# Block products by seven multiplications in the recurrence's projections as well

## The chip, the cores and the metric

The kernel runs as one program on one core of a Trainium2 chip. The metric is the time on the device of one execution, in microseconds (us), the median of several. The core's engines run their own instruction streams and wait for each other on semaphores: TensorE (PE: matmuls and transposes), VectorE (DVE), ScalarE (ACT), GpSimd (POOL), and the DMA queues, all issued here by SyncE (SP). Matmul operands and other tiles lie in SBUF; matmuls write the eight banks of PSUM, each of 128 rows by 512 fp32 numbers.

## What is computed

One step of a decoder layer with d = 1024, for a prompt of 1024 tokens with 16 learned tokens ahead, and for 8 single sample tokens that carry their own state. The core of the reference:

```
xn   = rmsnorm(h, norm_pre)
proj = xn @ w_in                                   # (L, 1024) @ (1024, 10 * 1024)
q, fr, i_in, z_a, b_g, c_g, h_c, z_b, gate_a, gate_b = split(proj)
f    = lb + (1 - lb) * sigmoid(fr);  k = 1 - f;  qa = silu(q)
o    = hgrn_mix(qa, k, i_in, log f)                # 8 heads: S_t = diag(f_t) S_{t-1} + k_t v_t^T ; o_t = q_t^T S_t
o    = rmsnorm(o, hgrn_norm) * silu(z_a);          y_a = o @ w_a
u    = c_g * h_c;  conv = causal width-3 depthwise convolution of u
y_b  = (b_g * conv * silu(z_b)) @ w_b
out  = (sigmoid(gate_a) * y_a + sigmoid(gate_b) * y_b) @ w_o
h    = h + rmsnorm(out, norm_post)
```

Outputs are h for prompt and sample tokens, the recurrence's last states and the convolution's last inputs.

## The kernel before, in words

**Layout.** Channels lie on the partitions and tokens on the free axis. The 1048 tokens are two halves of 524 columns (even 128-token chunks, odd chunks; 4 sample tokens and 8 learned ones at each end). Every fp32 operand of a large product is held as two fp32r parts, a high part (cast on ACT, L85) and the low rest (subtraction, on DVE unless told otherwise, L86: `split`). One block product is three matmuls, high-high, high-low and low-high (`mm3`, L109 to L111). The normalised input lies in SBUF as four blocks b00, b01, b10, b11 (channel half, token half), each as four 128-row pieces.

**Stages.** (1) A prelude loads, normalises and transposes the input (`prep`, L171 on PE) between the four projections of head 0. (2) For head m, a generator `hgrn(m)` of 19 steps is woven into `projections(m + 1)`: four sections of w_in (i, f, q, z), each of four column chunks with 8 pieces and three matmuls, so 4 x 4 x 24 = 384 matmuls per head. `weave` puts a step of the recurrence behind every so many half chunks. Head 7 runs beside four plain gate sections of the same size. (3) Two more plain gate sections run beside `block_sums`, which forms from the four blocks, high and low added on POOL (L592), subtracted on DVE (L595 to L600) and split again, the factors t1 to t4 of Winograd's form of the 2 x 2 block product. (4) `strassen` computes 21 pairs of sections by that form: seven block products in place of eight. The pairs are those of the convolution branch (c and h; b and z_b, eight each) and five pairs of gates. Per product j and pair, POOL and DVE prepare an operand (sums of weight blocks in `add`, L628 to L631; split in `operand`), three products ahead of its use; results pile up in PSUM banks pa, pb, pc, are saved to SBUF (`sc`, L667) or added from there (DVE, from PSUM, L711 to L768). (5) Two products with w_a and w_b, the output product and the residual.

**The recurrence.** One head's steps: two transposes of i (V, L235) and a small one; a front of DVE work on K, X (silu of q) and F (L260 to L263, with a split) that ends in two sums on PE (L271, L272) and one more (L361); seven levels, each with a copy on ACT (L364), four matmuls (L366), two products and one masked write on DVE (L368, L369, L374); then transposes of K, the states (L420 on DVE), the reads (L431, L433), a norm (squares on ACT, L436; root on POOL, L77 and L78; scaling on DVE, L441) and two transposes out (L447, L448). The sample tokens' states are updated in levels 1 to 6 (L316 to L346).

**What sets the order.** Each engine runs its instructions in the order of the program after scheduling; a tile of a pool waits until the last user of its buffer is done. Buffers: 6 operand buffers w, 4 raw weight buffers wr, two buffers each for X, F, K, ZS, 4 + 4 PSUM banks.

## Time and profile before

| | |
|---|---|
| median of 3 runs | 1327.33 us (1325.76 to 1327.61) |
| profiled execution, its own time | 1323.88 us |
| its span, first to last instruction | 1322.1 us, mean granted TensorE clock 0.997 |
| PE busy | 1293.5 us (98%) |
| DVE, ACT, POOL busy | 771.5 (58%), 433.0 (33%), 295.2 us (22%) |
| chain of waits by engine | PE 90%, DVE 6%, POOL 1%, DMA 1%, ACT 1% |

The profile comes from one execution, whose own time is 1.8 us above its span and 3.4 us below the median of the runs. The page divides the span into 40 slices and gives the busy tenths of each engine in them; a window view does the same for stretches that one names. The chain of waits is followed back from the last instruction: at each step to what released it. A line of a helper (L86, L109) stands for all its callers, so groups are told apart by tiles.

### The profile page before, as it was taken

The page shows a single profiled execution, that of the slowest core. Times are in us where ns is not written, and L with a number is a line of the kernel's source. Part 1 is how long each engine was busy: PE and PEld are TensorE (multiplying, and loading weights), DVE is VectorE, ACT ScalarE, POOL GpSimd, SP SyncE. Part 2 cuts the span into 40 slices and gives each one's busy share as a digit, 9 for nine tenths or more (in the row PEclk, how much of TensorE's full clock was granted, in tenths as well). Part 3 has the DMA queues.
Part 4 walks back from the last instruction along what each step waited for, and adds up shares of the span by engine and source line. Part 5 has one row for each costly group of instructions (what it writes and reads, how often), then busy time and mean ns, then how long its engine had stood idle before and what let it go on. Part 6 is the DMA issues. An engine that isn't in the chain of part 4 may idle for free.

```text
span 1322.1 us, 24885 instructions
## 1 busy us (share of the span) xinstructions
PE 1293.5 (98%) x10409; PEld 1259.5 (95%) x10409; DVE 771.5 (58%) x1336; ACT 433.0 (33%) x959; POOL 295.2 (22%) x372
## 2 busy tenths in 40 slices
PE   6999999999999999998999999999999999999997
PEld 5999999999999999998999999999999999999876
DVE  5397767776767676659655656655544523535052
ACT  6233333233232323234333334333445402213031
POOL 4121110202020201067554344353330000000010
PEclk9999999999999999999999999999999999999999
DMA  9022212131312121222212222213324833521141
GB/s 274 19 80 67 81 51 81 51 96 36 112 45 87 51 81 51 97 83 64 66 49 80 65 66 77 64 52 97 124 85 150 301 98 113 176 89 57 32 146 48
DMA packets 134590, 117.07 MB, mean 89 GB/s; under 512 B 3953, under 2 KB 119770, under 8 KB 134478
## 3 DMA queue, kind: packets, MB, share of 16 engines
q1 hardware_dynamic: 134478, 115.49, 28.1%
q8 instruction: 81, 1.33, 0.4%
q14 instruction: 31, 0.25, 0.1%
HBM read 89.48 MB, written 25.96 MB: 87 GB/s over the span
## 4 chain that ended last, share of the span: by engine, by line
PE 90%; DVE 6%; POOL 1%; DMA 1%; ACT 1%; issue 1%; SPq 0%; DVEq 0%; POOLq 0%; ACTq 0%
PE g L109 19%; PE g L110 18%; PE g L111 18%; PE h L111 8%; PE h L110 8%; PE h L109 8%; PE h L366 3%; PE h L433 1%; PE h L431 1%; PE h L414 1%; DVE w L86 1%; PE h L171 1%; PE h L447 1%; PE h L397 1%; DMA it<-in_x_prompt_dram 0%
## 5 line engine op out<-in xcount | busy, mean ns | idle before, releaser
L85 ACT CAST w<-wr 128x512 fp32r<-128x512 f32 (+1 forms) x116 | 94.8, 817 | 221.4 <-PE h L110 93.9
L86 DVE TENSOR_TENSOR w<-wr,w 128x512 fp32r<-128x512 f32 (+1 forms) x114 | 127.0, 1115 | 58.5 <-ACT w L85 58.5
L109 PE MATMUL g<-b00h,w 128*128 128x256 f32 (+1 forms) x448 | 131.8, 296 | 5.5 <-ACT z L564 5.1
L110 PE MATMUL g<-b00l,w 128*128 128x256 f32 (+1 forms) x448 | 128.2, 286 | 0.0
L111 PE MATMUL g<-b00h,w 128*128 128x256 f32 (+1 forms) x448 | 128.0, 286 | 0.0
L109 PE MATMUL g<-b10h,w 128*128 128x256 f32 (+2 forms) x440 | 125.8, 286 | 0.0
L110 PE MATMUL g<-b10l,w 128*128 128x256 f32 (+2 forms) x440 | 124.7, 283 | 0.0
L111 PE MATMUL g<-b10h,w 128*128 128x256 f32 (+2 forms) x440 | 124.4, 283 | 0.0
L109 PE MATMUL g<-b01h,w 128*128 128x256 f32 (+3 forms) x416 | 119.4, 287 | 0.0
L110 PE MATMUL g<-b01l,w 128*128 128x256 f32 (+3 forms) x416 | 117.9, 283 | 0.2 <-DVE b01l L86 0.2
L111 PE MATMUL g<-b01h,w 128*128 128x256 f32 (+3 forms) x416 | 117.8, 283 | 0.0
L109 PE MATMUL g<-b11h,w 128*128 128x256 f32 (+3 forms) x384 | 112.1, 292 | 0.0
L110 PE MATMUL g<-b11l,w 128*128 128x256 f32 (+3 forms) x384 | 108.8, 283 | 0.0
L111 PE MATMUL g<-b11h,w 128*128 128x256 f32 (+3 forms) x384 | 108.7, 283 | 0.0
L109 PEld LDWEIGHTS g<-b00h,w 128*128 128x128 f32 x448 | 86.0, 193 | 8.8 <-ACT z L564 5.4
L110 PEld LDWEIGHTS g<-b00l,w 128*128 128x128 f32 x448 | 86.1, 192 | 0.8 <-DVE b00l L86 0.2
L111 PEld LDWEIGHTS g<-b00h,w 128*128 128x128 f32 x448 | 86.0, 192 | 0.0
L109 PEld LDWEIGHTS g<-b10h,w 128*128 128x128 f32 x440 | 83.0, 189 | 0.4 <-issue 0.2
L110 PEld LDWEIGHTS g<-b10l,w 128*128 128x128 f32 x440 | 83.0, 189 | 0.1
L111 PEld LDWEIGHTS g<-b10h,w 128*128 128x128 f32 x440 | 82.9, 188 | 0.0
L110 PEld LDWEIGHTS g<-b01l,w 128*128 128x128 f32 x416 | 78.5, 189 | 0.6 <-DVE b01l L86 0.6
L109 PEld LDWEIGHTS g<-b01h,w 128*128 128x128 f32 x416 | 78.6, 189 | 0.1
(631 smaller groups left out, 3990.1 us busy)
## 6 DMA issues: line engine op xcount, KB each, us to landing
wr<-in_w_in_dram SPq DMA_DIRECT2D x79, 512.0 KB
oz<-z SPq DMA_DIRECT2D x8, 516.0 KB
ga<-z SPq DMA_DIRECT2D x8, 516.0 KB
ob<-t SPq DMA_DIRECT2D x8, 516.0 KB
gb<-z SPq DMA_DIRECT2D x8, 516.0 KB
z<-ga SPq DMA_DIRECT2D x8, 516.0 KB
z<-gb SPq DMA_DIRECT2D x8, 516.0 KB
sin<-in_state_hgrn_dram SPq DMA_DIRECT2D x8, 512.0 KB
```

Source lines behind the costliest of these rows:

```text
L85: act.copy(hi, src)
L86: (eng or vec).tensor_tensor(out=lo, in0=src, in1=hi.bitcast(F32), op=ALU.subtract)
L109: pe.matmul(pt, wh, xh, start=first, stop=False, skip_group_check=onto)
L110: pe.matmul(pt, wh, xl, start=False, stop=False, skip_group_check=onto)
L111: pe.matmul(pt, wl, xh, start=False, stop=last, skip_group_check=onto)
L171: pe.transpose(pt[:, 128 * k:128 * k + rows], src, ident[0:rows, 0:rows])
L366: pe.matmul(pt[:, 128 * j:128 * j + 128], kms[:, ko + 128 * j:ko + 128 * j + 128], comp(X, 128 * j + B, nb // 4, HL - B, B), start=True, s ...
L397: pe.transpose(pt[:, 128 * j:128 * j + 128], K[:, c0:c0 + 128], ident)
L414: pe.matmul(pt[:, 128 * j:128 * j + 128], KT[:, 128 * i:128 * i + 128], V[:, 128 * i:128 * i + 128], start=True, stop=True)
L431: pe.matmul(o, A[:, c:c + 128], V[:, c:c + 128], start=True, stop=False)
L433: pe.matmul(o, X[:, cx:cx + 128], states[t], start=False, stop=True)
L447: pe.transpose(pt[:, 128 * j:128 * j + 128], onb[:, 512 * g + 128 * j:512 * g + 128 * j + 128], ident)
```

## The change

All seven factors of the input are formed in the prelude and stay in SBUF (s0 to s6, high and low). The recurrence's projections of heads 1 to 7 become pairs too, (i, f) and (q, z), and so do all gates: one stream of 38 pairs (14 of heads, 8 of gates, 16 of the convolution branch) runs through `strassen`, and `weave` puts the steps of `hgrn(m)` between its chunks, 28 chunks per head. Head 0 stays plain. To make room there are now three operand buffers w, two wr, and one each for F, K and i (X and ZS keep two); operands are prepared two products ahead; PSUM is split into two banks ga, two banks gb and four for the recurrence. In the head pairs the low parts of three of seven operands are made on POOL, and so is the product of q's silu (three of four chunks from SBUF sums); K is one ACT instruction. The sample tokens' state update leaves `hgrn`; its inputs are kept, and its 64 steps run between the chunks of the convolution's pairs.

```
-    psg = ctx.enter_context(tc.tile_pool(name="psg", bufs=4, space=bass.MemoryType.PSUM))
+    psg = ctx.enter_context(tc.tile_pool(name="psg", bufs=2, space=bass.MemoryType.PSUM))
...
-    BUFS = {"x": 2, "f": 2, "k": 2, "zs": 2, "z": 2, "w": 6, "wr": 4, "cs": 2, "sc": 2, "st": 5}
+    BUFS = {"x": 2, "zs": 2, "w": 3, "wr": 2, "sm": 3, "cs": 2, "sc": 2, "st": 5}
...
+    def whole(h, l, out):
+
+        pool.tensor_tensor(out=out, in0=h.bitcast(F32), in1=l.bitcast(F32), op=ALU.add)
...
+                if (kk, h) == (0, 1):
+                    r = slot("sm", 512)
+                    rv = cap(r, 0, [[n, 4], [1, n]])
+                    whole(cap(b11[0], c0, here), cap(b11[1], c0, here), rv)
+                    vec.tensor_tensor(out=rv, in0=src, in1=rv, op=ALU.subtract)
+                    src = rv
+                split(src, cap(hi, c0, here), cap(lo, c0, here))
...
+    def q_out(m, h, c0, n, pt, s):
+        out = of_head(m, "x", h, c0, n)
+        y = added(pt, s)
+        sg = sigmoid(y, n)
+        (vec if s is None else pool).tensor_tensor(out=out, in0=y, in1=sg, op=ALU.mult)
...
+        K = slot("k")
+        act.activation(out=K, in_=F, func=AF.Copy, scale=-1.0, bias=1.0)
+        for i, t in enumerate((F, X, ZS)):
+            pool.tensor_copy(cap(smpv, 32 * m + 8 * i, [[4, 2], [1, 4]]), cap(t, 512, [[HL, 2], [1, 4]]))
...
+    t2, t3, t4 = factor(2), factor(4), factor(5)
+    for k in range(4):
+        ab, c = slot(("kt", "s")[k % 2], 2 * HL), slot("sc", HL)
+        a, b = ab[:, 0:HL], ab[:, HL:2 * HL]
+        whole(*at(b22, k), a)
+        whole(*at(t1, k), b)
+        vec.tensor_tensor(out=a, in0=a, in1=b, op=ALU.subtract)
+        split(a, *at(t2, k))
+        whole(*at(b11, k), b)
+        vec.tensor_tensor(out=b, in0=a, in1=b, op=ALU.subtract)
+        split(b, *at(t3, k))
+        whole(*at(b21, k), c)
+        vec.tensor_tensor(out=c, in0=c, in1=a, op=ALU.subtract)
+        split(c, *at(t4, k))
+        if k == 0:
+            groups(gi(1, 1), gf(1, 1))
+        if k == 1:
+            groups(gq(1, 1), gz(1, 1))
...
-    for m in range(7):
-        weave(projections(m + 1, tiles), 32, run_hgrn(m), N_HG, 1 if m else 2)
...
-    weave(gates_plain(0, 1, 2, 3), 32, run_hgrn(7), N_HG)
...
-    weave(gates_plain(4, 5), 16, block_sums(), 16)
...
-                sa, sb_ = (slot(t, 1024) for t in (("kt", "s"), ("a", "ee"))[p % 2])
-                s1, s2, s3, s4 = sums[p] = sa[:, 0:512], sa[:, 512:1024], sb_[:, 0:512], sb_[:, 512:1024]
+                s1, s2, s3 = sums[p] = [slot("sm", HL)[:, 0:512] for _ in range(3)]
...
+                s1, s2, s3 = sums.get(p, (None,) * 3)
+                src = (quad(p, 0, 0), quad(p, 0, 1), s2, s1, s3, quad(p, 1, 1), s2)[j]
                 w = ops[i] = slot("w", 1024, F32R)
-                split(src, w[:, 0:512], w[:, 512:1024])
+                split(src, w[:, 0:512], w[:, 512:1024], pool if j in pairs[p][2] else vec)
+                if j == 2:
+                    pool.tensor_tensor(out=s2, in0=quad(p, 0, 1), in1=s2, op=ALU.subtract)
 
         load(0)
-        load(1)
+        operand(0)
+        operand(1)
         add(0)
-        for i in range(3):
-            operand(i)
...
-        for p, (_, chunks, evac, end) in enumerate(pairs):
-            b1, b2 = (gbank, hbank) if p % 2 == 0 else (hbank, gbank)
-            pa, pb, pc = ([b() for _ in chunks] for b in (b1, b2, b1))
+        for p, (_, chunks, _, evac, end) in enumerate(pairs):
+            pa, pb = [abank(), abank()], [bbank(), bbank()]
+            held = {}
             for j in range(7):
                 i = 7 * p + j
-                if j == 0 and p:
+                if j == 3:
+                    pc = [bbank(), bbank()]
                     load(p + 1)
-                if j == 1:
+                if j == 6:
                     add(p + 1)
-                operand(i + 3)
+                operand(i + 2)
                 w = ops.pop(i)
-                dst = (pa, pb, pa, pc, pa, pa, pc)[j]
+                dst = (pa, pb, pa, pc, pa, pa, pc)[j] if j > 2 else (pa, pb, pa)[j]
+                onto = j in (2, 4, 5, 6)
+                if j in (0, 2, 4):
...
+    def head_pairs(m):
+        def pair(secs, outs, n):
+            return (tuple(sec_of(x, m) for x in secs), chunks_of(n), (1, 3, 5),
+                    lambda r, h, c0, w, pt, s: outs[r](m, h, c0, w, pt, s), lambda: None)
+        return [pair((2, 1), (i_out, f_out), HL), pair((0, 3), (q_out, z_out), HY)]
...
+    stream_of = [p for m in range(1, 8) for p in head_pairs(m)]
+    stream_of += [gate_pair(8, m, ga_d) for m in (0, 2)]
+    stream_of += [f(m) for m in range(8) for f in (u_pair, b_pair)]
+    stream_of += [gate_pair(8, m, ga_d) for m in (4, 6)] + [gate_pair(9, m, gb_d) for m in (0, 2, 4, 6)]
+    stream = strassen(stream_of, tail)
+    for m in range(8):
+        weave(stream, 28, hgrn(m), N_HG, 0 if m else 2)
+    cx = conv_context()
+    qz = slot("kt", 256)
+    pool.memset(qz, 0.0)
+    weave(stream, 14 * 16, sample_steps(), 64)
+    drain(stream)
```

The mask construction, the tail of the kernel and the products with w_a, w_b, w_o do the same work with other tiles.

**Where instructions stand.** First PE behind the prelude, at the start of head 0's recurrence. Before, the sums of that recurrence (L271, L272, of kt and s by ones) stand amid a plain section on all four blocks:

```order
L110 MATMUL g<-b00l,w 128x256
L111 MATMUL g<-b00h,w 128x256
L271 MATMUL h<-kt,ones_r 128x512
L272 MATMUL h<-s,ones_r 128x512
L271 MATMUL h<-kt,ones_r 128x512
L272 MATMUL h<-s,ones_r 128x512
L109 MATMUL g<-b10h,w 128x256
L110 MATMUL g<-b10l,w 128x256
L111 MATMUL g<-b10h,w 128x256
L109 MATMUL g<-b10h,w 128x256
```

With the change, the same sums (L276, L277) and the next one (L326) stand ahead of the first matmuls on factor t2 (s2h, s2l), the third product of the first pair:

```order
L110 MATMUL ga<-s0l,w 128x268
L111 MATMUL ga<-s0h,w 128x268
L276 MATMUL h<-kt,ones_r 128x512 x2
L277 MATMUL h<-s,ones_r 128x512 x2
L326 MATMUL h<-kt,ones_r 128x512
L109 MATMUL ga<-s2h,w 128x256
L110 MATMUL ga<-s2l,w 128x256
L109 MATMUL ga<-s2h,w 128x268
L110 MATMUL ga<-s2l,w 128x268
L327 MATMUL h<-kt,ones_r 128x512
```

So t2's product, and all that follows it, comes behind matmuls that need the front of head 0's recurrence on DVE.

Second, DVE in the same place. Before, the front of head 0 (L260, L262, L86 into s, L263, L368) runs among the mask constructions (L544 to L546), and nothing of the input's blocks is formed here:

```order
L260 TENSOR_TENSOR u<-k,x 128x1024
L213 SCALAR_TENSOR_TENSOR zs<-g,vecs,cs 128x260
L262 TENSOR_TENSOR x<-x,f 128x2x512
L546 TENSOR_TENSOR masks<-cs 128x512
L86 TENSOR_TENSOR s<-u,kt 128x1024
L544 TENSOR_SCALAR cs<-cs 128x512
L545 TENSOR_SCALAR cs<-cs 128x512
L263 TENSOR_TENSOR u<-k,x 128x512
L546 TENSOR_TENSOR masks<-cs 128x512
L368 TENSOR_TENSOR k<-k,f 128x256x2
L544 TENSOR_SCALAR cs<-cs 128x512
L545 TENSOR_SCALAR cs<-cs 128x512
```

With the change, the twelve subtractions (L517, L520, L523) and twelve splits (L89) of the factors come first, and the last of them, the masks and the front (L267 to L278) stand ahead of the split of the third operand (L89, w from sm, at the end):

```order
L517 TENSOR_TENSOR s<-s 128x524
L538 TENSOR_SCALAR sm<-sm 128x512
L523 TENSOR_TENSOR sc<-sc,s 128x524
L89 TENSOR_TENSOR s2l<-s,s2h 128x524
L520 TENSOR_TENSOR s<-s 128x524
L89 TENSOR_TENSOR s5l<-sc,s5h 128x524
L539 TENSOR_SCALAR sm<-sm 128x512
L89 TENSOR_TENSOR w<-wr,w 128x512
L89 TENSOR_TENSOR s4l<-s,s4h 128x524
```

```order
L89 TENSOR_TENSOR s<-u,kt 128x1024
L540 TENSOR_TENSOR masks<-sm 128x512
L270 TENSOR_TENSOR u<-k,x 128x512
L538 TENSOR_SCALAR sm<-sm 128x512
L539 TENSOR_SCALAR sm<-sm 128x512
L278 TENSOR_TENSOR a<-h,ident 128x512
L540 TENSOR_TENSOR masks<-sm 128x512
L278 TENSOR_TENSOR a<-h,ident 128x512
L89 TENSOR_TENSOR kt<-u,kt 128x512
L89 TENSOR_TENSOR w<-sm,w 128x512
```

Between the two pieces stand more masks and the front's first products; the operand of the third product has moved behind all of it.

Third, a head in the middle, on DVE and on POOL. In its levels on DVE, before, sample products (L318, L320) and plain evacuations (L201, L203) lie between the levels' products (L368, L369) and masked writes (L374):

```order
L203 TENSOR_SCALAR k<-f 128x256
L320 TENSOR_TENSOR sin<-sin,vb 128x1024
L369 TENSOR_TENSOR x<-x,ee 128x128x2x2
L374 COPY_PREDICATED a<-masks,h 128x128x2x2
L368 TENSOR_TENSOR k<-k,ee 128x32x2x8
L201 TENSOR_SCALAR f<-f,lbt 128x268
L326 COPY qz<-x 128x8
L203 TENSOR_SCALAR k<-f 128x268
L369 TENSOR_TENSOR x<-x,ee 128x64x2x4
L374 COPY_PREDICATED a<-masks,h 128x64x2x4
L368 TENSOR_TENSOR k<-k,ee 128x16x2x16
```

With the change, additions from PSUM (L204) and operand splits (L89) lie there instead:

```order
L204 TENSOR_TENSOR f<-gb,sc 128x268
L89 TENSOR_TENSOR w<-wr,w 128x512
L222 TENSOR_SCALAR f<-f,lbt 128x268
L222 TENSOR_SCALAR f<-f,lbt 128x256
L334 TENSOR_TENSOR x<-x,ee 128x64x2x4
L339 COPY_PREDICATED a<-masks,h 128x64x2x4
L333 TENSOR_TENSOR k<-k,ee 128x16x2x16
L222 TENSOR_SCALAR f<-f,lbt 128x268
L334 TENSOR_TENSOR x<-x,ee 128x32x2x8
L339 COPY_PREDICATED a<-masks,h 128x32x2x8
L333 TENSOR_TENSOR k<-k,ee 128x8x2x32
L204 TENSOR_TENSOR it<-gb,sc 128x256
```

In its last part on POOL, before, the roots of the norm (L77, L78) have nothing ahead of them but each other and the next head's small products:

```order
L77 TENSOR_SCALAR st<-st 128x4
L78 TENSOR_TENSOR st<-st,half 128x4
L77 TENSOR_SCALAR st<-st 128x4
L78 TENSOR_TENSOR st<-st,half 128x4
L280 TENSOR_TENSOR k<-k,f 128x2x4
L285 TENSOR_TENSOR k<-k,em 128x2x2x2
```

With the change, the three sums of the next pair's weights (L563 to L565), which wait for a weight DMA, stand ahead of the roots (L80, L81), an operand and q's products (L229) around them:

```order
L229 TENSOR_TENSOR x<-sc,cs 128x256
L229 TENSOR_TENSOR x<-sc,cs 128x260
L89 TENSOR_TENSOR w<-wr,w 128x512
L563 TENSOR_TENSOR sm<-wr 128x512
L564 TENSOR_TENSOR sm<-sm,wr 128x512
L565 TENSOR_TENSOR sm<-wr 128x512
L80 TENSOR_SCALAR st<-st 128x4
L81 TENSOR_TENSOR st<-st,half 128x4
L80 TENSOR_SCALAR st<-st 128x4
L81 TENSOR_TENSOR st<-st,half 128x4
L89 TENSOR_TENSOR w<-wr,w 128x512
```

## Rows read from the trace of the kernel before

**Rows 1.** The page's top: span, busy time of each engine.
```profile
span 1322.1 us, 24885 instructions
...
PE 1293.5 (98%) x10409; PEld 1259.5 (95%) x10409; DVE 771.5 (58%) x1336; ACT 433.0 (33%) x959; POOL 295.2 (22%) x372
```

**Rows 2.** Windows: stretch; length; busy PE, PEld, DVE, ACT, POOL; PEclk; DMA; GB/s.
```profile
0.00:33.00 33.00, 21.28 (x132) 19.27 (x133) 19.07 (x34) 22.79 (x46) 15.63 (x28) 0.95 0.93 274
26.00:33.00 7.00, 6.84 (x43) 6.84 (x44) 6.00 (x14) 6.29 (x15) 4.30 (x6) 0.76 0.65 159
66.00:100.00 34.00, 32.20 (x262) 31.52 (x260) 32.80 (x55) 11.45 (x21) 8.94 (x10) 1.00 0.26 78
200.00:300.00 100.00, 100.00 (x847) 98.07 (x846) 70.86 (x119) 31.38 (x73) 10.39 (x26) 1.00 0.27 80
600.00:700.00 100.00, 93.88 (x766) 92.75 (x765) 71.98 (x116) 40.81 (x87) 53.45 (x58) 0.98 0.23 70
700.00:800.00 100.00, 100.00 (x837) 100.00 (x837) 60.12 (x109) 37.64 (x79) 44.54 (x53) 1.00 0.22 64
```

**Rows 3.** Waits of PE: what waited, for whom; us in total, times, longest.
```profile
PE h L171 <- DVE z L165: 8.0, 1, 8.0
PE g L109 <- ACT z L564: 5.1, 1, 5.1
PE h L366 <- DVE x L369: 3.4, 3, 1.6
PE h L171 <- DVE it L165: 1.5, 1, 1.5
```

**Rows 4.** POOL by line and shape: names, shapes, count; busy us, mean ns; idle before.
```profile
L78 POOL TENSOR_TENSOR st<-st,half 128x4 f32<-128x4 f32 x16 | 20.5, 1282 | 1.3
...
L629 POOL TENSOR_TENSOR a<-a,wr 128x512 f32<-128x512 f32 x10 | 13.2, 1322 | 0.1
...
L592 POOL TENSOR_TENSOR s<-b00h,b00l 128x524 f32<-128x524 f32 x2 | 2.6, 1318 | 0.0
```

**Rows 5.** DVE by line and shape, columns as in the group above.
```profile
L86 DVE TENSOR_TENSOR w<-wr,w 128x512 fp32r<-128x512 f32 x63 | 64.0, 1017 | 47.1 <-ACT w L85 47.1
...
L374 DVE COPY_PREDICATED a<-masks,h 128x512 f32<-128x512 uint8 x56 | 59.3, 1059 | 0.0
L369 DVE TENSOR_TENSOR x<-x,ee 128x512 f32<-128x512 f32 x48 | 33.0, 688 | 14.5 <-PE h L366 14.5
...
L86 DVE TENSOR_TENSOR w<-s,w 128x512 fp32r<-128x512 f32 x22 | 15.1, 688 | 17.0 <-ACT w L85 17.0
...
L260 DVE TENSOR_TENSOR u<-k,x 128x1024 f32<-128x1024 f32 x8 | 9.8, 1220 | 0.0
...
L749 DVE TENSOR_TENSOR sc<-h,sc 128x256 f32<-128x256 f32 x16 | 6.7, 421 | 7.5 <-ACT sc L667 7.5
```

**Rows 6.** Chain of waits, 585 to 612 us: start, length, what.
```profile
590.87 1.28 POOL s L592
...
592.17 1.79 DVE u L595
593.96 1.73 DVE sin L86
595.69 1.74 DVE kt L596
597.43 1.73 DVE w L86
...
600.90 0.61 DVE u L595
```

**Rows 7.** Tile b11l: splits of the input; durations, first and last start.
```profile
L86 DVE TENSOR_TENSOR b11l<-h,b11h x6: 158/680/681, 27.2 to 52.8; 128x512 fp32r<-128x512 f32 x4, 128x16 fp32r<-128x16 f32 x1, 128x32 fp32r<-128x32 f32 x1
```

**Rows 8.** Tile oz: heads' results going out; durations, first and last start.
```profile
L556 SPq DMA_DIRECT2D oz<-z x8: 338/339/365, 141.0 to 580.6; - x8
```

**Rows 9.** Chain of waits, 630 to 645 us.
```profile
633.56 3.79 DMA wr<-in_w_in_dram
```

586 lines of the change are left out of this document (269 added, 317 removed).

## The prediction

> **What bounds the kernel now.** I read the page's top first: PE is busy in 1293.5 of 1322.1 us, DVE in 771.5, POOL in 295.2 [rows 1]. Then the busy time by stretches [rows 2]: in an ordinary hundred microseconds of the heads PE is full and DVE at 71, and in the pairs PE is full too, beside DVE at 60 and POOL at 45. Only three stretches lose anything: the first 33 us (11.7 idle), 66 to 100 us (1.8) and 600 to 700 us (6.1). The table of waits names them [rows 3]: transposes that wait for the prelude's DVE (8.0 and 1.5), one 5.1 us wait at the first pair behind the block sums, and 3.4 us in all for the recurrence's levels. The kernel is bound by the number of matmuls that PE is given, with 28.6 us of idle time in all. So the saving can be counted; what has to be found is where PE, with less to do, begins to wait.
>
> **Matmuls that go.** A plain pair of sections is 2 x 4 x 24 = 192 matmuls, a pair by seven products 7 x 2 x 12 = 168. Seventeen pairs change (14 of heads, 3 of gates): 408 fewer. In the pairs' stretch PE runs 837 matmuls in 100 us [rows 2], 0.1195 us each, so 408 x 0.1195 = **-48.7 us**. All other matmuls stay in number; the sample tokens' move.
>
> **The block sums' stall.** In 600 to 700 us PE is idle for 6.1 us and the granted clock is 0.98 [rows 2]: the factors and the first operands were late. The stretch is gone: **-6.5**, the clock's part included.
>
> **The prelude.** The work itself stays: 16 additions on POOL, 24 operations on DVE (four subtractions fewer, and those of t1 sit in the preparation). Before, 192 matmuls of plain gates hid most of it. How fast does it go? POOL alone needs 1.32 us for one addition [rows 4], DVE 0.69 for one operation of the same size (a split of 512 columns) [rows 5]. Together they don't overlap: in the chain, as long as POOL is adding, a DVE operation comes every 1.73 us (592.17, 593.96, 595.69, 597.43), and once POOL is done every 0.61 [rows 6]. So one POOL addition costs DVE about 1.1 us. Sixteen such pairs are 28 us, the eight DVE operations left over 5, together 33. It can begin when the last chunk of the input is split. Before, that split starts at 52.8 us [rows 7]; 24 more matmuls now stand ahead of it (2.9), and the split of t1 needs an addition on POOL (1.3): 57. So t2 is complete near 87, the rest near 90. Behind it on DVE, ahead of the third operand, stand masks and shifts (about 14, some 6 us at 0.42) and the front of head 0's recurrence: three operations of 1024 columns at 1.22, six of 512 at 0.69 [rows 5], 8 us, more where POOL interferes. The third product starts at 105 to 110. PE has, behind the last transposes, 96 matmuls of head 0, the first two products (48) and the transposes of V, 18 us, and so runs dry near 76. That is 31 us of idle time, and in a cold clock after it (in 26 to 33 us, behind the first wait, 0.76 [rows 2]) 2 more; 3 that were lost there before go. Together **+31**. Bounds: if POOL's additions go at 1.32 and DVE hides entirely between them, t2 is there near 79 and the front follows sooner, +15; if the front of head 0 shares the ports with POOL's next seven operations at 1.1 each, +40. I take the middle, which is the rate the trace shows.
>
> The Trainium skill (SBUF — State Buffer, "SBUF: two separate sides") says that a DVE operation with two SBUF inputs and a GpSimd operation that reads SBUF exclude each other for the whole instruction. The spacing of 1.73 beside 0.61 agrees. By that rule the same price falls on every head, which is the slower rival below.
>
> **A head's stage.** From the first result out to the last are seven heads: (580.6 - 141.0) / 7 = 62.8 us each [rows 8], 384 x 0.1195 = 45.9 of it projections and 16.9 the recurrence. Now 336 x 0.1195 = 40.2, and the recurrence without the samples' matmuls about 15.5: PE needs 55.7. What does DVE need? At its clean prices [rows 5]: 34 operations of two SBUF inputs (0.69, three at 1.22) 25 us, seven masked writes 7.4 (mean 1.06), 18 evacuations and scalings at 0.42 about 7.5, the rest 2: 42 us, to which POOL adds. POOL now does 18 operations of two SBUF inputs per head, 512 columns wide or half: six low parts, eight sums, four products of q, at 1.3 [rows 4], and the roots. I see two places.
>
> *The levels.* From the last sum of the front to the sixth level PE has 9 chunks of 1.43 (12 matmuls) and six steps of the recurrence at 0.9 (16.9 over 19): 18.3 us. DVE's order there, up to the product that the sixth level needs, is 13 products and splits (9.0), five masked writes (5.3 by the mean), four additions and four scalings (3.3), two copies (0.5): 18.1 us. It is level without POOL. Six or seven POOL operations fall into the stretch. At 1.1 each, if every one met a DVE operation with two SBUF inputs, that would be 7 us; the trace of the pairs shows far less where DVE is not packed: splits of raw weights take 1.02 instead of 0.69 [rows 5], 0.33 x 63 = 21 us over 21 pairs, with some eight POOL operations each, or 0.12 per operation. Half of DVE's time here is such operations, against a quarter there. I take 0.3 to 0.4: 2 to 2.5 us, of which little is slack.
>
> *The end of a head.* The roots of the norm stand on POOL behind three sums that wait for a weight transfer. That transfer can start only when the low part of the last raw operand is made, as there are two raw buffers, and takes 3.8 us [rows 9]; then 3 x 1.5 and the roots at 1.28 each [rows 4]. On DVE the scaling by the root stands ahead of z's products, which free the two ga banks for the next pair. By the rows the roots come 11 to 13 us behind the start of the fourth product, the scaling is wanted at 14; one us is left. A slower transfer or two contended sums would make 1 to 2 us.
>
> The front itself has cover: DVE 11 us from X to the sums, PE eight chunks and steps, 14. I take **2.0 us per head, 8 x 2.0 = +16**, with ends of 0 (no contention beyond the slack) and 5.4 (every POOL operation at 1.1: 42 + 18 x 1.05 = 61.1 against 55.7).
>
> **The pairs and the tail.** Samples add 64 steps, in DVE's free 40% and POOL's 55% [rows 2]; two operands ahead instead of three and two banks in turn can cost a copy's wait here and there: +2 (0 to 8). The tail's work is the same, and prices itself at nothing while PE's weights are ready.
>
> **Sum.** 1322.1 - 48.7 - 6.5 + 31 + 16 + 2 = 1315.9 us of span; the execution's own time was 1.8 above its span, so 1317.7. The median of the runs lies 3.4 above the profiled execution's 1323.9 (both in the table of times), so I put the median at 1321 and, rounded, forecast 1320.
>
> **Rivals.** *The saving comes through.* POOL's operations find DVE in operations that read PSUM, the heads cost nothing beyond their 55.7, the prelude 20: 1322.1 - 48.7 - 6.5 + 20 + 5.2 = 1292. For it: DVE is at 71 of 100 in the heads, and PE waited 3.4 us there in all. Against: in those stretches POOL did 10 to 15 us of work per hundred, where it will do nearly 50.
>
> *Slower: POOL's lock makes DVE the bound of the heads.* Each of the 18 POOL operations excludes DVE, a head takes 60 to 61 us, the stall is 4 to 5.4 us: 8 x 4 = 32 to 43, and the median 1337 to 1348. Rows 6 speak for it, the pairs against. It decides from the stall at which the sum is the old median: 1305 + 8s = 1327, s = 2.8 us per head; above 3.1 the kernel is slower by more than 0.2%.
>
> *Given back exactly.* Between 2.5 and 3.1 us per head, or a prelude near +40 at 1.5: within 1325 to 1330.
>
> **Chances.** The forecast's own case (1 to 2.5 us per head, prelude 25 to 38) 0.42, with a range of its own of 1308 to 1326; the saving comes through 0.18; slower 0.28; given back 0.12. Differences under 0.2% (1324.7 to 1330.0) can't be told from none here. Faster: 0.18 + 0.39 of the forecast's case = 0.57; the same 0.13; slower 0.30. The range reaches from the first rival's 1292 to 1343, in the upper part of the slower one.
>
> **What would show it.** In the profile of the changed kernel: 408 fewer than the 10409 instructions on PE [rows 1], the matmuls as far apart as before (the saving); PE idle for some 30 us between 70 and 110 us, with DVE and POOL alternating at 1.7 (the prelude); results of heads leaving every 57.7 us (55.7 would show the first rival, 60 or more the slower one); waits of PE for the products of the levels, and of the ga banks' first matmuls for z's product. No idle stretch near 600 us. I am wrong in the step on the prelude if PE idles there for less than 15 us, and in that on the heads if the spacing is 56 or under, or 60 and over.

## The result, and the profile after

The changed kernel takes 1394.58 us (median of 4 runs, 1393.06 to 1398.77), the kernel before, run beside it, 1327.43. The ratio is 1.051 (95% interval 1.049 to 1.054): slower by 67 us, where 1320 with a range of 1292 to 1343 was forecast, a saving of 7. The profiled execution has a span of 1391.3 us and took 1393.06.

The top of its page and the row of the granted clock in 40 equal slices (answer to [rows 1]):

```profile
span 1391.3 us, 24727 instructions
...
PE 1281.5 (92%) x10001; PEld 1236.1 (89%) x10001; DVE 866.5 (62%) x1417; ACT 495.4 (36%) x1128; POOL 525.4 (38%) x566
...
PEclk9977999999999999999999999999999999999999
```

The 408 matmuls are gone (10409 to 10001). But PE is busy for 12.0 us less, not 48.7, and idle for 109.8 instead of 28.6. So, against the forecast saving of 48.7, 36.7 us were lost in PE's busy time and 81.2 in its idle time: -48.7 + 36.7 + 81.2 = +69.2, the difference of the spans.

Windows of the kernel after, cut at its stages (columns as in [rows 2]: stretch, length, busy PE, PEld, DVE, ACT, POOL, granted clock, DMA, GB/s):

```profile
66.00:100.00 34.00, 18.61 (x121) 17.85 (x120) 33.15 (x41) 12.46 (x22) 25.19 (x22) 0.73 0.00 1
100.00:170.00 70.00, 58.21 (x420) 54.76 (x419) 57.41 (x91) 24.98 (x63) 33.83 (x34) 0.86 0.11 32
170.00:640.00 470.00, 435.53 (x3511) 424.12 (x3510) 368.12 (x574) 194.08 (x495) 234.83 (x260) 0.98 0.17 54
640.00:900.00 260.00, 234.70 (x1927) 230.33 (x1926) 154.22 (x272) 82.99 (x185) 121.23 (x125) 0.95 0.30 92
900.00:1391.30 491.30, 481.77 (x3651) 458.44 (x3649) 213.92 (x384) 148.59 (x294) 78.09 (x83) 1.00 0.36 117
```

A granted clock between 0.5 and 1 is a mixture of the two levels, 1.2 and 2.4 GHz. (1 - clock) x length is what a stretch loses to it at most: 9.2 + 9.8 + 9.4 + 13.0 = 41.4 us in the first four rows, some of it in idle time, where it costs nothing. The sum has the size of the 36.7, but that alone doesn't show that the clock is all of it (see the heads below). In each of these four rows PE also stands idle (15.4, 11.8, 34.5 and 25.3 us); before, PE was full in the heads at 1.00 [rows 2].

The heads' results going out (answer to [rows 8]; two transfers per head now, issued together):

```profile
L424 SPq DMA_DIRECT2D oz<-zs x16: 339/404/781, 172.5 to 615.1; - x16
```

They cut the span into three stages. Of the forecast's terms the 48 matmuls saved in the two pairs beside head 0 (5.7), its samples that leave (1.4) and its stall (2.0) are in the first row, with the 31; the block sums, one pair of gates (2.9) and the samples' own matmuls, 8 x 1.4, are in the third.

```
                            before    forecast    after    miss
to the first result          141.0       167      172.5     +5.5
seven heads               7 x 62.8  7 x 57.7   7 x 63.2    +38.6
from the last result on      741.5       745      776.2    +31
```

The same stages by PE's idle and busy time (window views of both kernels, us):

```
                            idle before   idle after   busy before   busy after
to the first result                14.7         40.5         126.3        132.0
seven heads                         0.5         34.5         439.1        408.1
from the last result on            13.4         34.8         728.1        741.4
```

So the 81.2 us of idle time are 25.8, 34.0 and 21.4 by stage. Busy time should have changed by about -7, -48.5 and +6.5 (with 1.2 us per head for the samples' matmuls, which the trace shows at 9.6 in all, not 1.4); it lies above that by some 12.5, 17.5 and 6.5.

PE's waits, kernel after (what waited, for whom; us in total, times, longest; answer to [rows 3]):

```profile
PE h L331 <- DVE x L334: 21.0, 13, 2.6
PE ga L109 <- DVE cs L705: 11.3, 5, 4.5
PE h L326 <- ACT kt L88: 10.5, 8, 2.3
PE h L164 <- DVE s4h L158: 9.4, 2, 7.9
PE ga L109 <- DVE u L204: 8.5, 1, 8.5
```

In the heads L331 is the recurrence's levels and L326 the last sum of its front; L705 is a product of the pairs behind them, L164 and L204 (here into u) belong to the prelude.

**The prelude** alternates as forecast. The chain of waits there (start, length, what; answer to [rows 6]):

```profile
68.19 1.73 DVE s2l L89
...
71.48 0.62 DVE s5l L89
...
72.71 1.73 DVE s L517
...
75.90 1.71 DVE sc L523
77.60 1.71 DVE s2l L89
```

1.7 us whenever POOL adds beside it, for operations that take 0.6 to 0.7 alone. The Trainium skill (SBUF — State Buffer, "SBUF: two separate sides") gives an exclusive lock as the reason. This trace agrees again, by 1.73 against 0.62.

The size of the stage is another matter. With 5.7 and 1.4 saved, and if head 0's stall is the 2.0 put to it, the growth of 31.5 us leaves 36.6 for the prelude, where 31 was forecast. It is made up in another way: PE's idle time grew by 25.8 (20.5 of 40 us between 70 and 110 us are idle, where some 30 were expected), its busy time by 12.5 more than the matmuls explain, at a granted clock of 0.73 and 0.86 in the first two rows above; the forecast had 28 net and 2.

**One head.** DVE's operations from the front of a head's recurrence to its states (start, length, engine, line, operation, tiles; idle time ahead in brackets):

```profile
364.95 1.23 DVE L267 TENSOR_TENSOR u<-k,x 128x1024 f32<-128x1024 f32 x1 [0.64 <-POOL x L229]
366.21 2.35 DVE L269 TENSOR_TENSOR x<-x,f 128x1024 f32<-128x1024 f32 x1
368.49 1.21 DVE L89 TENSOR_TENSOR s<-u,kt 128x1024 fp32r<-128x1024 f32 x1
369.74 1.80 DVE L270 TENSOR_TENSOR u<-k,x 128x512 f32<-128x512 f32 x1
...
379.80 2.47 DVE L339 COPY_PREDICATED a<-masks,h 128x512 f32<-128x512 uint8 x1
381.84 0.94 DVE L89 TENSOR_TENSOR w<-sm,w 128x512 fp32r<-128x512 f32 x1
...
382.97 1.51 DVE L334 TENSOR_TENSOR x<-x,ee 128x512 f32<-128x512 f32 x1
...
407.61 0.35 DVE L379 SCALAR_TENSOR_TENSOR s<-ee,h 128x128 f32<-128x128 f32 x1 [3.23 <-PE h L373]
```

From 365 to 399 us DVE has hardly a gap (1.6 us in all); then it idles again. The mean over a head hides that. PE's waits in the five heads from 172.5 to 490.7 us, all but 0.9 us, end with products of this stretch or their splits:

```profile
PE h L331 <- DVE x L334: 13.0, 8, 2.6
PE h L326 <- ACT kt L88: 6.1, 5, 1.2
PE h L327 <- DVE kt L89: 4.4, 5, 0.9
```

Nothing there waits for the roots, for z's product or for an operand. The same groups over the whole kernel (line, operation, shapes, count; busy us, mean ns; idle before):

```profile
L333 DVE TENSOR_TENSOR k<-k,ee 128x512 f32<-128x512 f32 x48 | 41.3, 861 | 9.7 <-ACT u L329 9.6
L334 DVE TENSOR_TENSOR x<-x,ee 128x512 f32<-128x512 f32 x48 | 40.6, 845 | 3.7 <-PE h L331 3.6
L269 DVE TENSOR_TENSOR x<-x,f 128x1024 f32<-128x1024 f32 x8 | 17.7, 2207 | 0.2
L270 DVE TENSOR_TENSOR u<-k,x 128x512 f32<-128x512 f32 x8 | 12.5, 1558 | 0.2
```

L334 was 688 ns before, as L369 there [rows 5]. L269 has the size of L267, which takes 1.23 above, and L270 took 829 ns before, as L263 there.

**The pairs.** A stretch of the chain of waits behind the heads, before PE starts the fourth product of a pair (on s3) at 790.26, behind a wait of 2.35 us for L204:

```profile
779.27 1.86 POOL ee L750
...
781.20 1.62 issue
782.82 0.43 DVE sc L667
...
783.32 1.12 POOL u L653
...
784.98 1.25 POOL sm L575
...
786.32 0.56 POOL so L80
...
786.96 2.02 POOL so L81
...
789.09 0.19 DVE w L89
```

L750 and L80 to L81 are a sample step's product and root on POOL, and a sum for the next pair stands between them. DVE, and behind it PE, come after that queue.

### The profile page after: what moved, and what is told of

It reads as the page before. It is cut to its first block, busy times and chain, and to the rows that moved or that the text cites. A ratio compares the mean times of both kernels' runs of the same rounds, so it can differ in the third digit from the quotient of the medians.

```text
span 1391.3 us, 24727 instructions
## 1 busy us (share of the span) xinstructions
PE 1281.5 (92%) x10001; PEld 1236.1 (89%) x10001; DVE 866.5 (62%) x1417; ACT 495.4 (36%) x1128; POOL 525.4 (38%) x566
## 4 chain that ended last, share of the span: by engine, by line
PE 59%; DVE 16%; POOL 9%; issue 6%; DMA 4%; ACT 2%; POOLq 0%; DVEq 0%; ACTq 0%
PE gb L109 7%; PE ga L109 7%; PE gb L110 7%; PE gb L111 7%; PE ga L111 7%; PE ga L110 7%; PE h L110 3%; PE h L109 3%; PE h L111 3%; DVE w L89 3%; PE h L331 2%; DVE a L339 2%; DMA wr<-in_w_in_dram 2%; DVE k L333 2%; DMA a<-in_state_hgrn_dram 1%
## 5 line engine op out<-in xcount | busy, mean ns | idle before, releaser
L88 ACT CAST w<-sm 128x512 fp32r<-128x512 f32 x152 | 94.3, 622 | 162.8 <-PE gb L111 120.5
L89 DVE TENSOR_TENSOR w<-sm,w 128x512 fp32r<-128x512 f32 x138 | 106.4, 771 | 58.8 <-ACT w L88 58.4
L563 POOL TENSOR_TENSOR sm<-wr 128x512 f32<-128x512 f32 x38 | 53.9, 1419 | 213.3 <-DMA wr<-in_w_in_dram 193.6
L109 PE MATMUL ga<-s0h,w 128*128 128x256 f32 (+3 forms) x344 | 104.9, 305 | 29.6 <-DVE cs L705 11.3
L109 PE MATMUL gb<-s1h,w 128*128 128x256 f32 (+3 forms) x344 | 100.7, 293 | 0.9 <-ACT v L472 0.9
L110 PE MATMUL ga<-s0l,w 128*128 128x256 f32 (+3 forms) x344 | 100.7, 293 | 0.0
L109 PE MATMUL gb<-s6h,w 128*128 128x256 f32 (+3 forms) x328 | 97.1, 296 | 3.6 <-DVE it L663 2.7
L109 PE MATMUL gb<-s3h,w 128*128 128x256 f32 (+3 forms) x328 | 95.4, 291 | 5.2 <-DVE sc L204 3.8
L89 DVE TENSOR_TENSOR w<-wr,w 128x512 fp32r<-128x512 f32 x86 | 73.7, 857 | 40.2 <-ACT w L88 39.0
L110 PE MATMUL gb<-s1l,w 128*128 128x256 f32 (+3 forms) x344 | 98.7, 287 | 0.0
L110 PE MATMUL gb<-s6l,w 128*128 128x256 f32 (+3 forms) x328 | 95.0, 290 | 0.0
L111 PE MATMUL ga<-s0h,w 128*128 128x256 f32 (+3 forms) x312 | 91.5, 294 | 2.3 <-DVE w L89 2.3
L110 PE MATMUL gb<-s3l,w 128*128 128x256 f32 (+3 forms) x328 | 93.2, 284 | 0.0
L111 PE MATMUL gb<-s6h,w 128*128 128x256 f32 (+3 forms) x304 | 88.2, 290 | 0.0
```

The costliest lines, as they stand in the source:

```text
L88: act.copy(hi, src)
L89: (eng or vec).tensor_tensor(out=lo, in0=src, in1=hi.bitcast(F32), op=ALU.subtract)
L109: pe.matmul(pt, wh, xh, start=first, stop=False, skip_group_check=onto)
L110: pe.matmul(pt, wh, xl, start=False, stop=False, skip_group_check=onto)
L111: pe.matmul(pt, wl, xh, start=False, stop=last, skip_group_check=onto)
L563: pool.tensor_tensor(out=s1, in0=quad(p, 1, 0), in1=quad(p, 1, 1), op=ALU.add)
```

## The experiments

Each ran beside the kernel before, whose medians lie between 1325.3 and 1328.3 us; "gain" is the difference of the run's median to the 1394.58 of the kernel after, and so known to some 2 us. In a cut edit, "..." stands for lines left out.

**Samples left out** (the sample tokens' recurrence isn't computed):

```
+    pool.memset(smpz, 0.0)
...
-    weave(stream, 14 * 16, sample_steps(), 64)
+    for _ in range(14 * 16):
+        next(stream, None)
```

> The changed kernel with the 64 steps of the sample tokens' state left out (no state update, no read, nothing in their place). Their own matmuls are some 7 us. Theory: these steps stand in DVE's queue between the pairs' evacuations and wait there for a state transfer (DVE waits 14.9 us in all for it), for POOL's product (12.2) and its roots (10.3), so that PSUM banks come free late and PE waits, then finds a clock of one half: the time falls by 30 to 38 us, and PE is full between 640 and 900 us. Rival: the pairs lose because only two banks take turns and operands are two ahead: then only the steps' own 7 to 10 us go.

1353.79 us, ratio 1.021 (1.019 to 1.024), gain 41. 9.6 of it are the samples' own matmuls (152 instructions of PE in the trace of the kernel after); 31 is what their steps cost beyond that, by standing where they stand. PE is busy in 254.81 of the 260 us from 640 to 900, at a clock of 1.00. The pairs' loss hangs on these steps and hardly on the two banks.

**POOL out of the heads' pairs** (the block sums are left out and raw blocks taken as operands, the low parts are copies, so other values come out):

```
...
+                if j in pairs[p][2]:
+                    act.copy(w[:, 0:512], src)
+                    act.copy(w[:, 512:1024], src)
...
```

> The changed kernel with POOL's eight weight sums and six low parts per head left out: the operands of the head pairs are raw weight blocks, and three low parts of each pair are a second copy on ACT (values are other ones, sizes and counts of matmuls the same). DVE does exactly what it did. Theory (each POOL operation with SBUF inputs shuts DVE out, some 7 us per head, on the path to PE): heads' results come 56 to 58.5 us apart instead of 63.2, and the time falls by 33 to 50 us. Rival (DVE's own 42 us and the order of its waits are too much for 55.7 us of PE): the spacing stays at 61 or more and the time falls by less than 15 us.

1343.17 us, ratio 1.014 (1.012 to 1.016), gain 51. Results of heads leave from 156.6 to 563.0 us, 58.1 apart. But that is a mean: the first five distances, beside pairs that have the edit, are 57.1 each; the last two, which reach into the gates' pairs with POOL's sums as before, are 59.1 and 61.5. So the five heads are to be compared, in the kernel after (first row, 63.6 apart) and in this run (second row):

```profile
172.50:490.70 318.20, 293.53 (x2332) 285.49 (x2331) 252.45 (x391) 130.40 (x336) 165.59 (x181) 0.97 0.14 44
156.60:442.10 285.50, 281.11 (x2333) 277.44 (x2333) 216.08 (x391) 147.47 (x365) 54.58 (x111) 1.00 0.16 49
```

Fourteen POOL operations per head cost 6.5 us of spacing, 0.47 each: 4.1 us of PE's idle time (4.9 to 0.9 per head) and 2.5 of its busy time (58.7 to 56.2). The granted clock explains at most 0.03 x 318.2 = 9.5 of the 12.4 us of busy time; what makes the rest the traces don't say. DVE's 78 operations per head are the same ones and take 50.5 us beside POOL's, 43.2 without: 7.3 us longer. The front of a head, from L267 to the split of its last operand, takes DVE 11.2 us instead of 13.5, the packed stretch 29.6 instead of 34 to 36, and the one wait of PE that is left in the five heads is at the levels:

```profile
PE h L331 <- DVE x L334: 4.4, 5, 0.9
```

The edit takes the waits for the sums off POOL's queue as well, but PE waited for no operand and no root in these heads. Over the whole kernel DVE's operations are back near their clean prices:

```profile
L334 DVE TENSOR_TENSOR x<-x,ee 128x512 f32<-128x512 f32 x48 | 34.0, 708 | 4.3 <-PE h L331 4.3
...
L270 DVE TENSOR_TENSOR u<-k,x 128x512 f32<-128x512 f32 x8 | 6.7, 835 | 0.2
```

**Three factors not formed** (other blocks of the input stand in for t2, t3 and t4):

```
-        vec.tensor_tensor(out=a, in0=a, in1=b, op=ALU.subtract)
-        split(a, *at(t2, k))
...
+    factors = [b11, b21, b22, t1, b11, b21, b22]
```

> The changed kernel with the forming of the factors t2, t3, t4 left out (16 additions on POOL, 24 operations on DVE; three other blocks stand in their place in all products). Theory (the forming, then masks and the front of head 0, leave PE idle and then at half clock between 63 and 150 us): the time falls by 40 to 50 us, of which 15 or so are the clock's. Forecast's own price: 31. Rival (the masks and the front of head 0 hold PE anyway): 15 to 20 us.

1366.91 us, ratio 1.032 (1.030 to 1.034), gain 27.7; the first result leaves at 143.8, 28.7 earlier. My theory of 40 to 50 fell. In the stage up to the first result 18.4 us of PE's idle and 10.2 of its busy time go. The masks and head 0's front, which the prediction's 31 holds too, are still there: 28.7 is the forming alone.

**The recurrence's steps at other chunks of the pairs**, the levels two chunks apart:

```
+    AT = (1, 2, 4, 5, 6, 8, 10, 12, 14, 16, 18, 19, 21, 22, 23, 24, 25, 26, 27)
...
-        weave(stream, 28, hgrn(m), N_HG, 0 if m else 2)
...
```

> The changed kernel with the recurrence's 19 steps set at other chunks of the stream: the seven levels two chunks apart (1.5 before), the steps behind them closer. Nothing is added or left out. Theory (DVE is packed only in the front and the levels, and idle for 8 to 10 us in the last third of a head): heads' results come 59.5 to 61.5 us apart instead of 63.2, and the time falls by 13 to 28 us. Rival (DVE and POOL together bound the whole head): no change within 5 us, or slower where the closer steps wait for each other.

1380.83 us, ratio 1.042 (1.040 to 1.044), gain 13.8: heads 61.9 apart, a mean of some 61 in the first five and 65.3 in the last. The wait at L331 falls from 21.0 to 5.9 us, that at L326 rises from 10.5 to 18.0: half of it moves to the front. The density of the levels is a part of the stall; DVE is short in the front too.

**The head pairs' POOL work onto DVE**, six low parts and four products of q per head (all four chunks of q are on POOL):

```
-            return (tuple(sec_of(x, m) for x in secs), chunks_of(n), (1, 3, 5),
+            return (tuple(sec_of(x, m) for x in secs), chunks_of(n), (),
...
```

> The changed kernel with the six low parts and the four q products per head on DVE, not on POOL (POOL keeps the sums). DVE gets 10 operations more, 6 of 0.69 and 4 of 0.42, 5.8 us per head. If POOL's operations cost DVE 0.4 each, as leaving 14 of them out says (5.1 us per head), the ten gave 4 back: heads' results come some 1 to 3 us further apart than 63.2 and the time rises by 8 to 22 us. If POOL's operations shut DVE out for their whole length (1.1 each, 11 us), the spacing falls by 4 to 5 us and the time by 30 or more.

1389.61 us, ratio 1.049 (1.046 to 1.051), heads 62.8 apart; hardly told apart from the kernel after. Neither theory's number: DVE is busy for 53.0 us in each of the first five heads, 2.5 more than 50.5, for ten operations more. For the spacing such an operation costs about the same whether POOL does it beside DVE or DVE itself.

**The masks first**, their tile and loop of shifts at the start instead of behind the factors:

```
-    masks = const.tile([128, 7, 4, 128], U8, name="masks")
...
+    masks = const.tile([128, 7, 4, 128], U8, name="masks")
```

> The changed kernel with the constant masks (19 DVE operations, two on POOL) made in the first 20 us, where DVE waits for the input. Theory (DVE is the chain between 63 and 110 us, so every operation there counts): the time falls by 6 to 12 us, the clock's part included. Rival (POOL's additions set the pace of that chain and the masks lie in its gaps): within 3 us.

1386.79 us, ratio 1.048 (1.044 to 1.051), gain 7.8, as expected by the medians (three of its four runs; the fourth, which is the profiled one, took 1395.06). In that trace the first result leaves at 163.9, 8.6 earlier, the transposes' wait at L164 grows from 9.4 to 15.7 us, and what was gained is lost behind it.

**The samples' transfers a head earlier, in two pairs of buffers:**

```
-        sin, vb = slot("a", 1024), slot("ee", 1024)
+        sin, vb = slot(("a", "s")[m % 2], 1024), slot(("ee", "f")[m % 2], 1024)
...
+                loads[m + 2] = sample_load(m + 2)
```

> The changed kernel with the same sample steps, but each token state's two loads issued a whole head of steps ahead into alternating buffers, POOL's product put first, and the last product one step behind the roots that it needs. Theory (DVE waits there for a transfer, for POOL's product and for the roots, and the pairs' evacuations stand behind it): of the 41 us that leaving these steps out saved, some 8 to 10 are their own matmuls and DVE work; 20 to 32 come back, and PE is full (over 255 of 260 us) between 640 and 900 us. Rival (the steps' volume on DVE and POOL is what costs): less than 10 us.

1389.64 us, ratio 1.049 (1.045 to 1.054): not told apart from the kernel after. POOL's product also comes a step earlier here, and the last product a step later. A miss: the transfers' latency alone isn't it.

**The same, issued where SP has nothing to wait for**, ahead of the step that sends the state out:

```
...
+        if m < 7:
+            loads[m + 1] = sample_load(m + 1)
...
```

> The changed kernel with the sample steps' transfers issued where nothing of SP's queue waits for them: loads half a head's steps ahead into buffers that have long been free, the state's way out two steps behind its last write, so that the weights' loads behind them on SP go out at once; volume, POOL's and DVE's work as before. In the runs so far the weights' loads stood on SP behind these transfers (waits of 5 to 12 us), and POOL, which waits for the weights 71.8 us in that stretch, holds q-like products of the pairs behind its sums. Theory (SP's queue): PE is busy 250 of 260 us between 640 and 900 us (234.7), and the time falls by 18 to 28 us. Rival (DVE and POOL volume of the steps, about 8 us of DVE per head): within 8 us.

1385.56 us, ratio 1.045 (1.043 to 1.048), gain 9, half of the least that was expected and close to the rival's 8. POOL waits less for raw weights from 640 to 900 us (the kernel after had 71.8 in the same row):

```profile
POOL sm L563 <- DMA wr<-in_w_in_dram: 41.8, 9, 6.2
```

**Besides, the samples' product on DVE, and all their roots at once at the end:**

```
-        pool.tensor_tensor(out=cap(vb, 0, s3), in0=cap(vb, 0, s3), in1=over(3), op=ALU.mult)
+        vec.tensor_tensor(out=cap(vb, 0, s3), in0=cap(vb, 0, s3), in1=over(3), op=ALU.mult)
...
+    pool.tensor_tensor(out=cap(smpm, 0, s88), in0=cap(smpm, 0, s88), in1=cap(half, 0, [[0, 8], [1, 8]]), op=ALU.pow)
```

> The changed kernel with the sample transfers off SP's queue and, besides, nothing of the sample steps on POOL: the state's product by k on DVE (1.2 us per head), the sums of the norm gathered and all roots taken at once at the end. With the transfers alone the pairs' stretch came to 240.7 us of PE in 260, and DVE still waited for POOL there (roots 16.5, product 11.0), POOL itself standing behind weight loads. Theory (DVE waiting for POOL, with the pairs' evacuations behind it): PE busy over 250 of 260 us, the time 1362 to 1372 us. Rival (what is left is the steps' own volume): within 6 us of 1385.

1379.78 us, ratio 1.039 (1.037 to 1.040), gain 14.8; missed by 8, and the time is one that the rival allowed (within 6 us of 1385). The windows decide between them: from 640 to 900 us PE is up to 250.23, as expected (240.72 in the run above); from 900 to 1000 it has only 89.44 (96.94 there). The one root, at 955.9, holds POOL for 10.6 us with a product of the pair behind it, and PE's wait for that product is new:

```profile
L837 POOL TENSOR_TENSOR smpm<-smpm,half 128x64 f32<-128x64 f32 x1 | 10.6, 10563 | 0.0
```

```profile
PE ga L110 <- DVE cs L706: 9.3, 1, 9.3
```

POOL's wait for raw weights, meanwhile, was 83.0 us from 640 to 900.

**Besides, roots in eight pieces, and two more raw buffers for every second pair's weights:**

```
+    RAW = {17 + 2 * m: ("x", "zs") for m in range(8)}
...
+                raws[p] = [load_weight(w, t) for w, t in zip(pairs[p][0], RAW.get(p, ("wr", "wr")))]
...
+        pool.tensor_tensor(out=ms, in0=ms, in1=half, op=ALU.pow)
+        for _ in range(4):
+            next(stream, None)
```

> The changed kernel with the sample steps off SP's queue and off POOL as before, the roots in eight pieces between later chunks instead of one (PE waited 9.3 us once behind it), and the raw weights of every second pair in other buffers (x, zs), so that four raw buffers stand under the convolution's pairs as in the kernel before. Theory (what is left of the pairs' loss is the one root, 10 us, and sums that wait 83 us for weights with evacuations behind them on POOL, 8 us): PE busy 255 or more of 260 us between 640 and 900 us, 97 or more of 100 behind it, the time 1360 to 1366. Rival (the two banks in turn): 1368 to 1374, the root alone.

1356.09 us, ratio 1.023 (1.021 to 1.025), gain 38.5, with every sample computed. The pairs are full, at full clock:

```profile
640.00:900.00 260.00, 260.00 (x2246) 257.64 (x2245) 176.89 (x314) 98.30 (x217) 126.28 (x133) 1.00 0.33 101
900.00:1000.00 100.00, 100.00 (x851) 99.66 (x851) 49.25 (x93) 42.64 (x95) 35.59 (x38) 1.00 0.27 91
```

From the last head's result to the end it takes 1353.2 - 616.2 = 737 us, where the forecast had 745. The two banks in turn and the two operands ahead, which this kernel still has, cost nothing there. POOL no longer waits for raw weights from 640 to 900 us. The windows also tell the two edits apart: 640 to 900 us ends before the one root stood, and the 9.8 us of idle time that went there belong to the raw buffers; of the 10.6 that went from 900 to 1000 us, 9.3 were the wait behind the root.

**Versions.** The first two compute (i, f) of all heads and both pairs of head 1 plainly, so that the factors can be formed beside heads 0 and 1; in the second each quarter of the forming is held back until a tile of head 1 or 2 is there, the masks stand later than in the first, and the sample steps are as in the run off the queue.

```
+    PLAIN = {(1, 0), (1, 1)} | {(m, 0) for m in range(2, 8)}
```

> A version made of what was found: masks first, samples early, the factors formed beside head 0's and head 1's recurrence, and in the heads only (q, z) of heads 2 to 7 by seven products; (i, f), and both pairs of head 1, plain, in the same stream. Against the kernel before 9 pairs save 24 matmuls each, 216 x 0.1195 = 25.8 us, and 6.5 at the block sums. A plain pair needs no sums on POOL, three splits and two additions fewer on DVE, for 24 matmuls (2.9 us) more on PE. Theory: PE needs 58.6 us per head, and DVE and POOL are light enough for a spacing of 59 to 60.5; the first result leaves at 150 us or sooner, the pairs lose 5: 1300 to 1318 us. Rival (seven factors' split operands and the recurrence can't share DVE at all): 1325 or more.

> The half-plain version with three things mended: masks made behind the even chunks of the input instead of ahead of the first (PE waited 15.7 us instead of 9.4 there), each quarter of the factors held back until a tile of head 1 or 2 is there (they ran ahead of head 0's front on DVE in spite of their place), and the sample transfers off SP's queue. Theory: first result at 146 us or sooner (168.6), heads 60.4 apart, the pairs full: 1310 to 1325 us. If the pairs still lose 20 us: 1330 to 1340.

1362.00 us, ratio 1.028 (1.026 to 1.030), and 1362.53, ratio 1.028 (1.026 to 1.030): both misses. In the first the forming came ahead of head 0's front (first result at 168.6). In the second the first result is out at 153.1, but the next head then takes 74.0 us instead of 59.6: the second result leaves at 227.1, in the first version at 228.2. The forming was moved, not hidden, and the pairs are as poor as before (242.93 of 260). Where it isn't formed and POOL has less to do, heads are 59.6 apart with PE idle for 0.4 us each.

The third keeps heads 1 to 3 plain and takes seven products only for (q, z) of heads 4 to 7 and for the gates; a quarter of the factors is formed beside each of heads 0 to 3, and the samples are as in the run with one root. The fourth adds roots in pieces and the four raw buffers, places three quarters earlier, and holds each back by an earlier column of the same tile.

```
-    PLAIN = {(1, 0), (1, 1)} | {(m, 0) for m in range(2, 8)}
+    PLAIN = {(m, 0) for m in range(1, 8)} | {(m, 1) for m in range(1, 4)}
```

> A version: masks where the changed kernel has them; heads 1 to 3 plain in the one stream, of heads 4 to 7 only (q, z) by seven products; a quarter of the factors formed beside each of heads 0 to 3 (held back by a tile of the next head); gates all by seven products; sample steps as in the run without POOL. 7 pairs save 24 matmuls each, 168 x 0.1195 = 20.1 us against the kernel before, and 6.5 at the block sums. Theory: heads 60.5 to 61.5 us apart with PE full, the first result near 147, the pairs full but for 5 us: 1305 to 1318 us. Rival (a prelude or samples that lose 20 us still): 1325 or more.

1342.74 us, ratio 1.011 (1.009 to 1.013). PE is full from 66 to 100 us (34.00 of 34), but the one root costs 9.3 us again, and a wait at a head's levels, beside which the last quarter is formed, 6.9: the miss.

> The version with quarters of the factors, with the roots in pieces, four raw buffers under the convolution's pairs, and the quarters held back by the first column of q's silu instead of its last chunk, so that they fall into the last third of a head and not into the front of the next (PE waited 7.6 us there once). Theory: 10 us of the root, 7 of the front, 5 to 8 of the weights: 1316 to 1324 us, faster than the kernel before by up to 1%. Rival (quarters and samples are paid in another place): 1328 or more.

1315.58 us (1315.34 to 1316.67, 5 runs), ratio 0.992 (0.991 to 0.994): 0.8% faster than the kernel before, clear of the interval. Its page and windows:

```profile
span 1313.6 us, 25026 instructions
...
PE 1278.6 (97%) x10241; PEld 1242.7 (95%) x10241; DVE 818.2 (62%) x1392; ACT 484.4 (37%) x1092; POOL 407.1 (31%) x490
```

```profile
66.00:100.00 34.00, 34.00 (x280) 33.71 (x280) 30.55 (x50) 14.25 (x27) 9.38 (x17) 1.00 0.16 48
100.00:170.00 70.00, 69.03 (x564) 67.40 (x564) 54.09 (x92) 27.30 (x67) 21.58 (x33) 1.00 0.13 40
170.00:580.00 410.00, 397.37 (x3246) 390.57 (x3245) 309.59 (x509) 168.68 (x431) 155.27 (x197) 0.99 0.18 56
```

It saves 168 matmuls, 20.1 us, and the block sums' 6.5; 10.9 us of this are kept. In its heads 5.1 us of idle time remain beside the last quarter, 4.0 beside the gates' pairs and under 1 in each of the others. The gain over the third version is behind the heads, which end within 1 us of each other in both: from the last result on it takes 737.9 us instead of 765.7. Tying the quarters to an earlier column gained nothing: the head beside the last of them takes 67.8 us, 67.4 in the third.

## Why the prediction was wrong

**Right.** The number of matmuls and their price; the stall of the block sums is gone; the prelude's alternation at 1.7 us. DVE's own work was well counted: 42 us per head were forecast and 43.2 are there without POOL's part, 11 and 11.2 for the front. The levels' share of the stall, about 2.0, is what the runs show too: 13.0 - 4.4 = 8.6 us of waits at L331 in five heads, 1.7 each.

**Right in part by luck: the prelude's +31.** It took 36.6, inside the bound of 40. The forecast put too much to idle time (28 net, 25.8 measured) and too little to busy time (2, some 12.5). The forming alone is worth 28.7 us by the run without it, the masks' place some 8 by the run with the masks first; the forecast put 6 to these.

**The step that failed first: a head's stage, "I take 2.0 us per head", by the sentence "The front itself has cover".** The measured stall is 63.2 - 55.7 = 7.5, 7.9 in the five heads compared above: PE idle for 4.9, busy for 58.7. The forecast set DVE's 11 us in the front against 14 of PE and so put POOL there at nothing. Without POOL's part PE doesn't wait in the front at all. With it L269 takes 2.2 us instead of 1.4 and L270 1.6 instead of 0.8, the front grows by 2.3 us, and PE waits (6.1 + 4.4) / 5 = 2.1 us per head there: the cover was some 0.2 us, not 3. The second place, the end of a head, cost PE nothing: it never waits there for z's product.

The rest of the 7.9 is 0.9 us of waits at the levels that are there without POOL's part, the 1.7 that come with it, 0.2 of small waits, 0.5 by which PE's own need was put too low (56.2 for 55.7), and 2.5 of longer matmuls, for which the forecast has no term in the heads. The price of one POOL operation, "0.3 to 0.4", holds for the idle time (4.1 / 14 = 0.29); with the busy time it is 0.47. But these are means over all fourteen operations of a head, where the forecast multiplied by six or seven. The slower rival had the mechanism, its point of decision (2.8) and its sign, and the idle part of 4.9 lies in its 4 to 5.4; it had no term for the longer matmuls.

**The second: "The pairs and the tail ... +2 (0 to 8)".** 31 us were lost. The cost was taken from shares of busy time (DVE's free 40%, POOL's 55%); what counted was what waits in which queue. A sample step has operations on DVE that wait for POOL or for a transfer, and the evacuations that free PE's banks stand behind them; its transfers stand on SP between those of the weights, for which POOL's sums wait; these sums stand behind its roots. Taking one link away gave little (5, 9), two 14.8, all of them with the two more raw buffers 38.5. The two banks and the two operands ahead, which the +2 was put to, cost nothing.

**The third: the clock, "2 more".** Lower clocks are in both of the above, and the forecast has a term for them in the prelude alone. PE's busy time came out 36.7 us too long, in stretches where PE had stood idle many times for a few us; on average an idle us came with 0.45 us of it: (81.2 + 36.7) / 81.2 = 1.45. That is no price for a single idle stretch. In the kernel after the first five heads have 3.8 to 5.9 us of idle time each at a clock of 0.97, the last two 5.0 and 4.8 at 1.00. Where a run filled a stretch, the clock there was 1.00 as well (the pairs: 0.95 in the kernel after, 1.00 in the run with four raw buffers). How much of the 36.7 is the clock stays open; in the five heads it is at most 9.5 of 12.4.

Nothing of the first rival is left: the saving was there, and each stage gave more than its part back.

## What to carry to other kernels

Where matmuls are traded for work on side engines, look at the longest dependent stretch of each stage, not at an engine's share of it, and count the other engine's operations into all of it: here the levels were priced so and the front, which stands just ahead of them in the same packed stretch, was not. A step that is moved is priced by what stands behind it on every queue it touches. Idle time of PE can bring a lower clock with it; allow for that in every stage that will idle. The saving can be taken only where the side engines have room, as in the last version, which does 168 matmuls fewer instead of 408 and is the only one here that gains.

## What the runs showed of the hardware

Roots on POOL grow with their columns: 0.57 us for 128x1, 1.05 for 128x4 (1.28 in the kernel before), 1.71 for 128x8 (means in the kernel after), 10.56 for 128x64 (the run with one root).

Beside fourteen POOL operations per head, DVE's products of two SBUF inputs grew (L334 from 0.71 to 0.85 us, L269 from 1.36 to 2.21), while its masked writes, whose data come from PSUM (L339), kept their 1.06 us with and without them.

Moving ten operations per head from POOL to DVE changed the spacing of heads by 0.4 us (63.2 to 62.8), although DVE itself needs some 6 us for them (six at 0.69, four at 0.42): beside a DVE as packed as here, POOL was hardly a second engine for operations of two SBUF inputs.

Much the same idle time came with different clocks: 5.3 us in one head at 0.97, 5.0 in another at 1.00 (kernel after).
